# Filling every SBUF pool up to a multiple of 256 bytes in a four-layer fp32r transformer kernel

## The chip, the cores and the metric

The kernel runs on one core of a Trainium2 chip. The metric is the device time of one execution in microseconds. Three runs of the kernel before took 4075.82, 4077.94 and 4079.65 us; their median, 4077.94 us, is the time before. Another execution was profiled; durations below are of that one.

## The reference

The kernel computes four transformer layers over 1024 rows of 1024 float32 values, one after the other: a layer of dilated window attention and a layer of multi-head latent attention (MLA), each with an adaptive scale, shift and gate from `c` and a layernorm behind it, and then two layers of a second block. Cut to the second block, in which most of the time lies:

```python
for l in range(2):
    h = rms_norm(x, norm_mix_pre[l])
    proj = h @ w_in[l]                       # 1024x1024 @ 1024x2560
    q_da, k_da, v_da, q_r, k_r, v_r, g_r, u_pool = jnp.split(proj, split_points, axis=-1)
    o_da = diff_attention(q_da, k_da, v_da, ...)   # 4 heads, two causal softmaxes subtracted
    o_ret = retention(q_r, k_r, v_r, g_r, ret_norm[l])
    o_pool = pool_mixer(u_pool, pool_w[l], pool_scale[l])
    mix = jnp.concatenate([o_da, o_ret, o_pool], axis=-1) @ w_out[l]   # 1024x1024
    x = x + rms_norm(mix, norm_mix_post[l])
    h = rms_norm(x, norm_mlp_pre[l])
    u = h @ w_up[l]                          # 1024x1024 @ 1024x5632
    uc = conv_b + sum(conv_w[j] * up[:, j:j + S] for j in range(3))   # up: u, two rows of zeros ahead
    gate, val = jnp.split(uc, 2, axis=-1)
    y = (gelu(gate) * val) @ w_down[l]       # 1024x2816 @ 2816x1024
    x = x + rms_norm(y, norm_mlp_post[l])
```

## The kernel before

**Products.** All large products are made from fp32r tiles. A float32 operand is split into a high part (`uh`, `wh`, `hh`, `yh`) and the rest (`ul`, `wl`, `hl`, `yl`), and a product is three matmuls into the same PSUM tile: high by low, high by high, low by high (`PASSES`). A matmul takes a stationary operand of up to 128 columns and a moving one of up to 512; in the trace's `out<-a,b` the first, `a`, is the stationary one. All matmuls go through `mm` (L151), transposes through `tr` (L156, with the identity `ident`).

**Stages.** `build` (L1889) runs phase A (dilated attention), phase B (MLA), and then twice `phase_mix` (projections, differential attention, retention, pooling, and the output product in `mix_tail`, L1666) and `phase_mlp` (L1740). The transposed activations of a stage are in a `UT` object (L98): `uh0`, `uh1`, `ul0`, `ul1`, each 128 x 4 x 8 x 128, named by the stage in which they are made: `uh_a` for dilated attention, `uh_n` for MLA and for the first mix layer, `uh_f` for the second, `uh_m` for the MLPs. In the MLP the up projection makes two halves of 512 rows per 128 columns of `w_up` (products `y<-uh_m,wh` or `g<-uh_m,wh`, 24 matmuls each, with the PSUM tags `y` and `g` in turn); the down projection, in groups of four 128-row pieces of `w_down`, takes `hh`/`hl` as the moving operand or the stationary one and the weights `wh`/`wl` as the other. TensorE's order in the MLP is written out by `pin` (each instruction is kept in program order); elsewhere the scheduler orders each engine's instructions.

**Memory.** A tile comes from a pool. Pools are opened and closed as on a stack, on the left side of each partition's SBUF (upward from its bottom) or on the right side (downward from its top), so a pool's address follows from the sizes of all pools open before it on that side. Left: `const` (the identity and other constants; opened first), `wraw` (raw weights `wr`), `ut`, and then a stage's own. Right: among others `pw` (L1895, three buffers for each of `wh` and `wl`), which holds the weights of both mix layers and both MLPs. A `TagPool` (L122) is a family of such pools, one for each tag, opened at a tag's first tile or by `reserve`. No size is rounded beyond 32 bytes, so small tiles (statistics, vectors of constants) shift all that is opened behind them.

**Queues.** Nearly all transfers are issued on the SP queue, in one order that the scheduler sets; a transfer waits for its data, its buffer and the ones ahead of it on the queue. In `mix_tail`, `load` fetches a piece `yr` of the stored mixer outputs `mixd`, which earlier stores (`mixd<-do` of differential attention, L1602) wrote.

Of the kernel before, what the change touches and what calls it, by code (L numbers as in the profile page):

```python
# [12 lines left out]
F32 = mybir.dt.float32  # L13
# [8 lines left out]
P = 128  # L22
# [75 lines left out]
class UT:  # L98


    def __init__(self, k, name):
        self.hi = [k.ut.tile([P, 4, KT, P], F32R, tag=f"uh{h}", name=f"uh{h}_{name}") for h in range(2)]
        self.lo = [k.ut.tile([P, 4, KT, P], F32R, tag=f"ul{h}", name=f"ul{h}_{name}") for h in range(2)]
# [4 lines left out]
    def lhs(self, part, t, kt):  # L108
        return (self.hi if part == 0 else self.lo)[t // 4][:, t % 4, kt, :]


class Pools:


    def __init__(self, rest, tags):
        self.rest, self.tags = rest, tags

    def tile(self, shape, dtype, **kw):
        return self.tags.get(kw.get("tag"), self.rest).tile(shape, dtype, **kw)


class TagPool:  # L122


    def __init__(self, k, ctx, name, bufs, side):
        self.k, self.ctx, self.name, self.bufs, self.side, self.pools = k, ctx, name, bufs, side, {}

    def reserve(self, *tags):
        for t in tags:
            self.pools[t] = self.k.pool(self.ctx, f"{self.name}_{t}", bufs=self.bufs, side=self.side)  # L130

    def tile(self, shape, dtype, **kw):
        t = kw.get("tag") or kw["name"]
        if t not in self.pools:
            self.reserve(t)
        return self.pools[t].tile(shape, dtype, **kw)


PASSES = ((1, 0), (0, 0), (0, 1))


class Kern:
# [26 lines left out]

    def tags(self, ctx, name, bufs=1, side="left"):  # L170
        return TagPool(self, ctx, name, bufs, side)

    def psum(self, ctx, left="", right=""):

        for side, tags in (("left", left), ("right", right)):
            for t in tags:
                self.ps.tags[t] = self.pool(ctx, "ps" + t, space=PSUM, side=side)
# [62 lines left out]
    def gemm_T_half(self, w, ut, half, ps, cols=slice(0, P), kts=range(KT)):  # L240
        for kt in kts:
            for n, (a, b) in enumerate(PASSES):
                self.mm(ps, w[kt][a][:, cols], ut.rhs(b, half, kt), start=(kt == 0 and n == 0),
                        stop=(kt == KT - 1 and n == 2))

    def gemm_N(self, ps, w, cols, lhs, kts=KT):
# [3 lines left out]
        for kt in range(kts):  # L250
            for a, b in PASSES:
                self.mm(ps, lhs(b, kt), w[kt][a][:, cols], start=(m == 0), stop=(m == 3 * kts - 1))
# [58 lines left out]
    def setup(self, ctx):  # L311
        nc = self.nc
        self.cp = self.pool(ctx, "const")
        self.wr = self.pool(ctx, "wraw")
        self.ut = self.pool(ctx, "ut")
        self.dr = self.pool(ctx, "dram", space=DRAM)
        self.ident = self.cp.tile([P, P], F32, name="ident")
        make_identity(nc, self.ident)
        self.xs = [self.dr.tile([S, D], F32, name=f"xs{j}") for j in range(2)]
        self.modd = self.dr.tile([4, 1024], F32, name="modd")  # L320
# [612 lines left out]
    def mla_heads(self, ctx, cr, lat, kbuf, rope, sgd, yT, rd, begin_tail):  # L933
# [27 lines left out]
        def quad_v(qd, t, ps):  # L961
            _, wv, vt, _ = quad[qd]
            ps = ps[:, :256].rearrange("p (h e) -> p h e", h=4)
            for n, (a, b) in enumerate(PASSES):
                self.mm(ps, lat[b][:, 2, t * P:(t + 1) * P], wv[a][:, 1], start=(n == 0), stop=(n == 2))
            self.split(vt[:, t, :, 0:64], vt[:, t, :, 64:128], ps)

        def pair_k(qd, pr, half, ps=None):
            wv = quad[qd][1]
            hs = slice(half * 512, (half + 1) * 512)  # L970
            ps = self.pp("g", 1) if ps is None else ps
            for n, (a, b) in enumerate(PASSES):
                self.mm(ps, wv[a][:, 0, pr * 2:pr * 2 + 2], lat[b][:, 2, hs], start=(n == 0), stop=(n == 2))
# [153 lines left out]
    def tail_finish(self, ctx, early, late, w_out, x_res, layer):  # L1127
# [7 lines left out]
        with ctx:  # L1135
# [22 lines left out]
            def product(t, side):  # L1158
# [8 lines left out]
                for j, (ks, rows) in enumerate(parts):  # L1167
# [5 lines left out]
                    for kt in ks:  # L1173
                        for n, (a, b) in enumerate(PASSES):
                            for h in range(2):
# [56 lines left out]
    def phase_mix(self, l, ut, x_res):  # L1232
        nc, i = self.nc, self.i
        w_in = i["w_in_2"][l]
        mixd = self.dr.tile([S, 1024], F32, name=f"mixd{l}")
        with ExitStack() as ctx:
            cw = ExitStack()
            wn = self.pw
            dp = self.tags(ctx, "dae")
            dp.reserve("dv0", "dv1", "dconst", "dc", "rp0", "rp1", "rp2", "rp3")  # L1240
            self.psum(cw, "tg")
            c1 = ExitStack()
            self.psum(c1, "", "xsv")
            rest = self.retention(self.tags(c1, "rt"), dp, wn, l, ut, w_in, mixd)

            def late_pool():
                c1.close()
                self.up = ExitStack()
                self.psum(self.up, "", "y")
                return self.tags(ctx, "da")  # L1250

            def begin_tail():
                w = self.load_w(wn, i["w_out_2"][l, 512:], 0, 1024, 3, cut=4)
                return w, {}, {}, []

            def load_y(early, h):
                y0 = early[1][h] = self.raw([P, 2, 512])
                nc.sync.dma_start(y0, mixd[:2 * P, h * 512:(h + 1) * 512].rearrange("(t p) n -> p t n", p=P))

            def turn_y(early, t, h):  # L1260
                yy = self.wr.tile([P, 2, 4, P], F32R, tag="wr", bufs=5, name=self.nm("wr"))
                tp = self.pp("g", 2, [P, 4, P])
                self.transposes(tp, early[1][h][:, t], 4)
                self.split(yy[:, 0], yy[:, 1], tp)
                early[2][t, h] = yy[:, 0], yy[:, 1]

            def products(early, t):
                w, _, yy, ps = early
                ps.append(self.pp("y", 2, [P, 1024]))
                self.out_product(ps[t], yy[t, 1], w, range(3), start=True)  # L1270

            def end(early, n):

                if n == -2:
                    load_y(early, 1)
                elif n in (-1, 0):
                    turn_y(early, n + 1, 1)
                    if n == 0:
                        load_y(early, 0)
                elif n in (1, 2):  # L1280
                    turn_y(early, n - 1, 0)

            early = self.diff_attention(dp, wn, l, ut, w_in, mixd, rest, late_pool, begin_tail, end, products)
        return self.mix_tail(cw, early, l, mixd, x_res)
# [40 lines left out]
    def retention(self, lp, dp, wn, l, ut, w_in, mixd):  # L1325
# [13 lines left out]
        def proj_pool(ti, half):  # L1339
            ps = self.pp("g", 2)  # L1340
            n = 0
            for kt in range(KT):
                for a, b in PASSES:
                    self.mm(ps, w_pool[ti][kt][a], ut.rhs(b, half, kt),
# [573 lines left out]
```

## Time and profile before

| | |
|---|---|
| median of three runs | 4077.94 us |
| profiled execution | 4074.51 us, span of its instructions 4072.7 us |
| mean granted TensorE clock | 0.978 of full speed |
| TensorE (PE) busy | 3848.7 us, 95% of the span, 21088 matmuls |
| VectorE (DVE) busy | 2455.7 us, 60% |
| ScalarE (ACT) busy | 1381.1 us, 34% |
| GpSimd (POOL) busy | 1089.9 us, 27% |
| DMA | 290.78 MB, mean 71 GB/s |

Busy time is that in which at least one instruction of an engine runs; matmuls are pipelined, so a printed duration holds the fill and drain of the array, and overlaps the next one's. What a matmul costs in a row of them is the distance from one start to the next. Times in the trace count from the start of the span. Stages: dilated attention to about 800 us, MLA to about 1551, mix layer 0 to 2028, its MLP to about 2820, mix layer 1 to 3306, its MLP to the end. PEclk is the granted clock of TensorE: 1.00 is 2.4 GHz, 0.50 is 1.2 GHz.

### The profile page before, as it was taken

The numbers are of one execution on the slowest core, as the hardware profiler recorded it, in microseconds if no ns is written. First come the engines' busy times: TensorE is split into PE (matmuls) and PEld (weight loads), VectorE is DVE, ScalarE is ACT, GpSimd is POOL, SyncE is SP. The second block draws the span as 40 slices with busy tenths as digits, with TensorE's granted clock in tenths as the row PEclk, the third lists the DMA queues.
The fourth block names the chain that finished last, engine by engine and source line by source line (L and its number), as shares of the span: only waits on it lengthen the run. The fifth ranks groups of instructions, "written<-read, shape, count | busy, mean of one in ns | idle before, by whom it ended". The sixth has DMA issues, their size and how long they took to land. (4 is left out here: it accounts for less than half of the span.)

```text
span 4072.7 us, 54330 instructions
## 1 busy us (share of the span) xinstructions
PE 3848.7 (95%) x21088; PEld 3265.4 (80%) x21088; DVE 2455.7 (60%) x4599; ACT 1381.1 (34%) x2938; POOL 1089.9 (27%) x1016
## 2 busy tenths in 40 slices
PE   7999998899999899999999999997999999999998
PEld 5778776788889778998778888886999778888886
DVE  6655567938887766588744444438568754343436
ACT  3434341127777532265311111113246431111111
POOL 1121212311122222233232222234134232323233
PEclk9999999999999999999999999998999999999999
DMA  6333324320111342101421111113111331111112
GB/s 239 99 93 81 100 68 149 90 71 17 28 36 30 93 126 86 42 30 53 142 70 47 47 47 47 47 52 115 47 45 37 117 98 42 52 42 52 42 52 83
DMA packets 300367, 290.78 MB, mean 71 GB/s; under 512 B 52107, under 2 KB 254739, under 8 KB 300110
## 3 DMA queue, kind: packets, MB, share of 16 engines
q1 hardware_dynamic: 294834, 268.23, 21.7%
q10 hardware_dynamic: 5276, 19.08, 1.6%
q8 instruction: 167, 2.74, 0.3%
q14 instruction: 90, 0.74, 0.1%
HBM read 240.26 MB, written 51.72 MB: 72 GB/s over the span
## 5 line engine op out<-in xcount | busy, mean ns | idle before, releaser
L203 POOL TENSOR_TENSOR wl<-wr,wh 128x1024 fp32r<-128x1024 f32 (+1 forms) x253 | 498.2, 1977 | 1461.5 <-DVE wh L199 1393.6
L199 DVE CAST wh<-wr 128x1024 fp32r<-128x1024 f32 x222 | 181.6, 819 | 688.9 <-PE y L151 312.4
L151 PE MATMUL y<-uh_m,wh 128*128 128x512 f32 x1056 | 420.4, 398 | 0.0
L151 PE MATMUL y<-uh_m,wl 128*128 128x512 f32 x1056 | 417.9, 396 | 2.2 <-DVE z L1643 1.7
L151 PE MATMUL y<-ul_m,wh 128*128 128x512 f32 x1056 | 419.2, 397 | 0.0
L1796 ACT ACTIVATE cv<-y,cw 128x1024 f32<-128x1024 f32 x66 | 79.8, 1209 | 776.9 <-PE y L151 776.9
L151 PEld LDWEIGHTS y<-uh_m,wl 128*128 128x128 f32 x1056 | 199.3, 189 | 52.5 <-DVE z L1643 2.2
L151 PEld LDWEIGHTS y<-uh_m,wh 128*128 128x128 f32 x1056 | 199.5, 189 | 48.7
L151 PEld LDWEIGHTS y<-ul_m,wh 128*128 128x128 f32 x1056 | 199.4, 189 | 47.6 <-DVE ul_m L191 0.7
L151 PE MATMUL g<-uh_a,wl 128*128 128x512 f32 x568 | 233.3, 411 | 0.2 <-ACT uh_a L419 0.2
L151 PE MATMUL y<-wo,yh 128*128 128x512 f32 x784 | 217.6, 400 | 15.6 <-ACT yh L1170 15.4
L151 PE MATMUL g<-ul_a,wh 128*128 128x512 f32 x568 | 226.6, 399 | 0.5 <-POOL ul_a L422 0.4
L151 PE MATMUL g<-uh_a,wh 128*128 128x512 f32 x568 | 225.6, 397 | 0.0
L151 PEld LDWEIGHTS y<-wo,yh 128*128 128x128 f32 x784 | 147.8, 191 | 48.4 <-issue 14.5
L191 DVE TENSOR_TENSOR pt<-t,pt 128x512 fp32r<-128x512 f32 x256 | 165.9, 681 | 22.5 <-ACT pt L190 20.8
L151 PE MATMUL y<-wl,hh 128*128 128x512 f32 x440 | 175.0, 398 | 0.0
L151 PE MATMUL y<-wh,hh 128*128 128x512 f32 x440 | 174.8, 397 | 0.0
L151 PE MATMUL y<-wh,hl 128*128 128x512 f32 x440 | 174.6, 397 | 0.0
L1007 DVE TENSOR_REDUCE nm<-s 128x1 f32<-128x1024 f32 x128 | 155.7, 1216 | 26.5 <-PE s L151 25.9
L151 PE MATMUL g<-wl,uh_n 128*128 128x256 f32 x576 | 166.1, 288 | 3.4 <-DVE dv L191 2.9
L151 PE MATMUL g<-wl,uh_f 128*128 128x256 f32 x576 | 166.1, 288 | 3.1 <-DVE dv L191 2.6
L151 PE MATMUL v<-pt,v 128*64 128x256 f32 (+1 forms) x1024 | 154.9, 294 | 11.1 <-DVE o L1042 11.0
(451 smaller groups left out, 10275.9 us busy)
## 6 DMA issues: line engine op xcount, KB each, us to landing
wr<-w_up SPq DMA_DIRECT2D x88, 512.0 KB, 3.9
wr<-ada_w SPq DMA_DIRECT2D x48, 512.0 KB, 5.5
wr<-w_down SPq DMA_DIRECT2D x44, 512.0 KB, 3.5
wr<-a_w_in SPq DMA_DIRECT2D x36, 512.0 KB, 4.5
wr<-w_in SPq DMA_DIRECT2D x24, 512.0 KB, 3.6
xs<-wr SPq DMA_DIRECT2D x16, 512.0 KB, 2.6
wr<-xs ACTq DMA_DIRECT2D x16, 512.0 KB, 3.7
wr<-w_in SPq DMA_DIRECT2D x32, 256.0 KB, 3.0
```

Source lines behind the costliest of these rows:

```text
L151: ins = self.nc.tensor.matmul(*args, **kw)
L191: nc.vector.tensor_tensor(lo, src, hi.bitcast(F32), OP.subtract)
L199: (self.nc.scalar.copy if act else self.nc.vector.tensor_copy)(hi, raw)
L203: (eng or self.nc.gpsimd).tensor_tensor(lo[..., cs], raw[..., cs], hi[..., cs].bitcast(F32), OP.subtract)
L1007: nc.vector.tensor_reduce(nm, sp, AX.X, OP.max, negate=True)
L1796: nc.scalar.activation(t, ps, AF.Identity, bias=cw[:, 3, c:c + 1], scale=cw[:, 2, c:c + 1])
```

## The change

Each pool of a `TagPool` is given a neighbour, `..._fill`, which holds one unused tile, as large as is missing from the pool's size to the next multiple of 256 bytes. Behind the constants on the left lies a fill of 192 bytes (`LEFT`), at the top on the right one of 224 (`RIGHT`), and one pool that is reserved but gets small tiles of its own sizes (`dconst`) has its fill written out, 224.

```diff
--- before.py
+++ after.py
@@ -122,21 +122,30 @@
 class TagPool:
 
 
+
     def __init__(self, k, ctx, name, bufs, side):
         self.k, self.ctx, self.name, self.bufs, self.side, self.pools = k, ctx, name, bufs, side, {}
+        self.fill = {}
 
     def reserve(self, *tags):
         for t in tags:
             self.pools[t] = self.k.pool(self.ctx, f"{self.name}_{t}", bufs=self.bufs, side=self.side)
+            self.fill[t] = self.k.pool(self.ctx, f"{self.name}_{t}_fill", side=self.side)
 
     def tile(self, shape, dtype, **kw):
         t = kw.get("tag") or kw["name"]
         if t not in self.pools:
             self.reserve(t)
+        fill = self.fill.pop(t, None)
+        if fill:
+            size = -(-math.prod(shape[1:]) * 4 // 32) * 32 * kw.get("bufs", self.bufs)
+            self.k.fill(fill, -size % ROUND)
         return self.pools[t].tile(shape, dtype, **kw)
 
 
 PASSES = ((1, 0), (0, 0), (0, 1))
+ROUND = 256
+LEFT, RIGHT = 192, 224
 
 
 class Kern:
@@ -169,6 +178,11 @@
 
     def tags(self, ctx, name, bufs=1, side="left"):
         return TagPool(self, ctx, name, bufs, side)
+
+    def fill(self, pool, size):
+
+        if size:
+            pool.tile([P, size // 4], F32, name=self.nm("fill"))
 
     def psum(self, ctx, left="", right=""):
 
@@ -311,6 +325,8 @@
     def setup(self, ctx):
         nc = self.nc
         self.cp = self.pool(ctx, "const")
+        self.fill(self.pool(ctx, "left"), LEFT)
+        self.fill(self.pool(ctx, "right", side="right"), RIGHT)
         self.wr = self.pool(ctx, "wraw")
         self.ut = self.pool(ctx, "ut")
         self.dr = self.pool(ctx, "dram", space=DRAM)
@@ -1238,6 +1254,7 @@
             wn = self.pw
             dp = self.tags(ctx, "dae")
             dp.reserve("dv0", "dv1", "dconst", "dc", "rp0", "rp1", "rp2", "rp3")
+            self.fill(dp.fill.pop("dconst"), 224)
             self.psum(cw, "tg")
             c1 = ExitStack()
             self.psum(c1, "", "xsv")
```

What it does to the addresses, as the built programs have them, bytes past a multiple of 256 at which a tile starts:

| tiles | before | after |
|---|---|---|
| `uh`, `ul` of all stages; `wr`; `hh`, `hl`; MLA's `kb`, `qh`, `ql`, `pt`, `v` | 64 | 0 |
| `wh`, `wl` of dilated attention and of MLA's gates (left) | 64 | 0 |
| `wh`, `wl` of both mix layers and both MLPs (`pw`, right) | 224 | 0 |
| `wo` and `yh`, `yl` at the end of dilated attention (right) | 224 and 224 | 0 and 0 |
| `wo` and `yh`, `yl` at the end of MLA (left) | 64 and 64 | 0 and 0 |
| `wo` and `yh`, `yl` of `mix_tail` (left) | 64 and 192 | 0 and 0 |
| `wh`, `wl` with `yh`, `yl` made by `turn_y` ahead of `mix_tail` | 224 and 64 | 0 and 0 |
| `dk` and `dq` of differential attention | 96 and 96 | 0 and 0 |
| `dv` and `dp` of differential attention | 64 and 0 or 96 | 0 and 0 |
| MLA's 416-column weights `wb` with `uh`, first and second half | 224, 96 with 64 | 0, 128 with 0 |
| `ident` (float32, with 128-column operands) | 128 | 128 |

Offsets within a tile are multiples of 512 bytes in all the 512-column products. Of these there are 11232 in fp32r; in 4128 both operands start at the same offset before, in 7104 they don't. After the change both start at 0 in all of them.

The instructions of TensorE, VectorE and ScalarE are the same, in the same order; on GpSimd two `memset`s change places. On the SP queue the order differs in three places. The first is in `mix_tail` of the first mix layer, where `yr` is a piece of `mixd` for one 128-row tile and `do` an output of differential attention. Before:

```order
L1684 DMA yr_20945<-mixd_14936 128x512
L1602 DMA mixd_14936<-do_20267 128x4x128
L1684 DMA yr_20734<-mixd_14936 128x512
L1684 DMA yr_20867<-mixd_14936 128x512
L1684 DMA yr_20994<-mixd_14936 128x512
```

After:

```order
L1701 DMA yr_21526<-mixd_15424 128x512
L1701 DMA yr_21665<-mixd_15424 128x512
L1701 DMA yr_21743<-mixd_15424 128x512
L1619 DMA mixd_15424<-do_20960 128x4x128
L1701 DMA yr_21792<-mixd_15424 128x512
```

Two `yr` loads now stand ahead of the store instead of behind it. The second place is the same spot of the second mix layer, with the same move. The third is where the second mix layer loads its tables (`rdec`, `rxz` for retention, `dcrope` and `dcgs` for differential attention; `wr` are raw pieces of `w_in`). Before:

```order
L1379 DMA rdec<-k_decay 128x512
L1456 DMA dcrope<-k_rope 128x128
L217 DMA wr_26664<-w_in 128x4x256
L217 DMA wr_26973<-w_in 128x4x256
L206 DMA dcgs<-diff_subln 128x128
L1381 DMA rxz<-k_xizeta 128x256
```

After:

```order
L1473 DMA dcrope<-k_rope 128x128
L220 DMA dcgs<-diff_subln 128x128
L231 DMA wr_27590<-w_in 128x4x256
L231 DMA wr_27912<-w_in 128x4x256
L1398 DMA rxz<-k_xizeta 128x256
L1396 DMA rdec<-k_decay 128x512
```

`rdec` has gone from the head of the six to their end, and `dcgs` ahead of the two weight loads.

## Rows read from the trace of the kernel before

**Rows 1.** Stages by window: busy us (xcount) of each engine, PEclk, DMA share, GB/s.

```profile
10.00:33.00 23.00, 14.25 (x51) 8.68 (x52) 19.45 (x17) 6.32 (x11) 0.00 (x0) 0.90 1.05 381
...
1551.00:1722.00 171.00, 163.79 (x1276) 158.34 (x1276) 97.30 (x269) 33.95 (x99) 35.56 (x37) 0.98 0.18 55
...
2028.00:2768.00 740.00, 734.64 (x3144) 589.58 (x3143) 317.42 (x331) 114.55 (x111) 222.17 (x93) 1.00 0.17 53
...
3306.00:4015.00 709.00, 704.15 (x3007) 565.57 (x3006) 291.58 (x280) 106.54 (x100) 206.55 (x86) 1.00 0.17 51
```

**Rows 2.** Chain of waits, a piece in the last MLP: start, us, what.

```profile
3349.90 22.40 PE y L151 x96
```

**Rows 3.** Timeline of PE, start of the first MLA block: start, us, instruction.

```profile
825.70 0.39 PE L151 MATMUL g<-ul_n,wh 128*128 128x512 f32 x1
...
831.82 0.39 PE L151 MATMUL g<-ul_n,wh 128*128 128x512 f32 x1
```

**Rows 4.** Timeline of PE, start of the first mix layer.

```profile
1576.75 0.40 PE L151 MATMUL g<-ul_n,wh 128*128 128x512 f32 x1
...
1585.85 0.40 PE L151 MATMUL g<-ul_n,wh 128*128 128x512 f32 x1
```

**Rows 5.** Stretches inside stages by window, same columns as the first group.

```profile
825.00:895.00 70.00, 70.00 (x310) 57.99 (x309) 15.11 (x24) 10.94 (x17) 16.21 (x8) 1.00 0.23 76
1560.00:1584.00 24.00, 24.00 (x170) 22.35 (x169) 18.60 (x55) 2.92 (x8) 9.52 (x6) 1.00 0.26 78
2060.00:2760.00 700.00, 700.00 (x2997) 562.78 (x2997) 290.26 (x270) 103.26 (x95) 204.62 (x86) 1.00 0.16 49
```

**Rows 6.** Timeline of PE, `wo` products: dilated block, then first mix tail.

```profile
629.83 0.62 PE L151 MATMUL y<-wo,yh 128*128 128x512 f32 x2
...
641.17 0.61 PE L151 MATMUL y<-wo,yl 128*128 128x512 f32 x2
...
1975.19 1.08 PE L151 MATMUL y<-wo,yh 128*128 128x512 f32 x4
1976.12 0.62 PE L151 MATMUL y<-wo,yl 128*128 128x512 f32 x2
```

**Rows 7.** PE by line and shape: xcount, busy us, mean ns, idle before, releaser.

```profile
L151 PE MATMUL y<-uh_m,wh 128*128 128x512 f32 x1056 | 420.4, 398 | 0.0
...
L151 PE MATMUL y<-wh,hh 128*128 128x512 f32 x440 | 174.8, 397 | 0.0
...
L151 PE MATMUL g<-wl,uh_n 128*128 128x256 f32 x576 | 166.1, 288 | 3.4 <-DVE dv L191 2.9 <-POOL wl L203 0.5
...
L151 PE MATMUL g<-uh_m,wh 128*128 128x512 f32 x352 | 139.6, 396 | 0.0
...
L151 PE MATMUL g<-wh,hh 128*128 128x512 f32 x264 | 104.6, 396 | 0.0
...
L156 PE MATMUL g<-ident,yr 128*128 128x128 f32 x96 | 14.4, 273 | 1.0 <-DMA yr<-mixd 0.6 <-issue 0.4
```

**Rows 8.** Timeline of PE, 256 columns: MLA values, then first mix layer.

```profile
1099.82 0.63 PE L151 MATMUL v<-pt,v 128*64 128x256 f32 x4
1100.29 0.39 PE L151 MATMUL s<-kb,ql 96*128 96x512 f32 x1
...
1569.77 0.28 PE L151 MATMUL g<-wh,ul_n 128*128 128x256 f32 x1
...
1575.46 0.28 PE L151 MATMUL g<-wh,ul_n 128*128 128x256 f32 x1
```

**Rows 9.** Timeline of the SP queue, loads in the first mix tail.

```profile
1945.92 5.50 SPq L1684 DMA_DIRECT2D yr<-mixd  x3
```

**Rows 10.** Timeline of PE, end of the first MLP, clock at half.

```profile
2795.27 0.63 PE L151 MATMUL y<-wh,hl 128*128 128x512 f32 x1
...
2796.13 0.61 PE L151 MATMUL y<-wh,hh 128*128 128x512 f32 x1
```

## The prediction, made before the changed kernel ran

> **What bounds the kernel now.** I read the table of stages first [rows 1]. In the long stages the reader is to see TensorE busy almost without a break: 734.64 us of 740 and 704.15 of 709 in the two MLP stages, 163.79 of 171 in the first differential-attention projections, while VectorE, ScalarE and GpSimd each stand below half of the MLP stages. The chain of waits says the same of the last MLP: it runs through matmul after matmul, 96 of them in 22.40 us, 233.3 ns each [rows 2]. So the time of one matmul, times some thousands, is the time of the kernel, and a change that alters no instruction can count only through what one instruction takes.
>
> The second view is the timeline of TensorE, read by the distance from one start to the next (the printed durations overlap and don't show it). The reader is to see that the same product, `g<-uh_n,wl / uh_n,wh / ul_n,wh`, 128x128 by 512 columns, has two speeds. At the start of the first MLA block 27 distances take 831.82-825.70 = 6.12 us, **226.7 ns** each [rows 3]; at the start of the first mix layer 39 take 1585.85-1576.75 = 9.10 us, **233.3 ns** [rows 4]. The granted clock is 1.00 in both [rows 5]. What differs by the table of addresses above: in the first stretch both operands start 64 bytes past a multiple of 256; in the second the `uh` operand starts at 64 and the weight at 224. I take "same offset" and "different offsets" as two classes. Two more rows bear that out with other tiles: `wo` with `yh`/`yl` of the dilated block, both at 224, take 641.17-629.83 = 11.34 us for 50, 226.8 ns [rows 6]; those of a mix tail, at 64 and 192, 0.93 us for 4, 232.5 ns [rows 6]. And the whole middle of the first MLP, where all pairs are 64 with 224, gives 700.00/2997 = 233.6 ns [rows 5].
>
> **The change part by part.** It adds no instruction to any engine. It moves SBUF addresses, and through them a few SP loads.
>
> *512-column products.* By the addresses, 7104 of 11232 stand in the different class before; after, all stand in the same class. By groups [rows 7]: `uh_m` with weights, 3 x 1056 and 3 x 352 (up projection); weights with `hh`/`hl`, 3 x 440 and 3 x 264 (down projection): 6336. The rest of the built program's pairs: 96 `uh_f`, 96 `uh_n`, 216 `wl/wh` with `yh/yl`, 72 with `wr`: together 6816 at 64/224. Taking 233.4 - 226.7 = 6.7 ns each: 45.7 us. Then 288 `wo` pairs at 64/192, 232.5 - 226.8 = 5.7 ns: 1.6 us. Sum 47.3. Of it 6336 lie in MLP stages where TensorE waits 5.4 and 4.8 us in all [rows 1]; the few per cent in the tails may be lost to waits, so I count **46.3 us**. The cover that could take it back there is another engine: VectorE, busiest of them, has 317.42 of 740 us and would stand at 317 of some 718, so none is late next.
>
> *256-column products.* 3456 pairs of weights with `uh` [rows 7] go from 224/64 to the same class, and 288 `dv,dp` too. In the different class 48 distances take 5.69 us, 118.5 ns; in the same class (`pt,v`, both at 64) 4 take 0.47 us, 117.5 ns [rows 8]. By the rows' two decimals the difference is 1.0, give or take 2.5 ns. These stages wait for VectorE for a part (97.30 of 171 us busy, TensorE 163.79 [rows 1]), so of 3744 x 1.0 = 3.7 us I take **2 us**. The bounds are 0 and 3744 x 3.5 = 13 us, where every pair gains the most that the rows leave room for.
>
> *416- and 384-column, 128-column products.* 192 of 416 columns change, half of them to a difference of 128 bytes; 192 x 6.7 = 1.3 us is the most, 0 the least; I take 0, since half keep different offsets. The 128-column ones with `ident` still differ by 128 after: 0.
>
> *Loads past the stores on SP.* In both mix tails two `yr` loads of t = 2 and 3 go ahead of a `mixd<-do` store. Before, three loads come at 1945.92 and land by 5.50 us later [rows 9]; the transposes that read `yr` cost TensorE 1.0 us of idle time over both layers [rows 7], and that is the most to be had: 0 to 1.0, I take **0.5**. Behind the moved loads on SP stands the store and then a `yr` load that is read after three more tiles; nobody is waiting for it. The three small table loads that change places at the start of the second mix layer are read by retention long after the projections: 0, at most the 1 us or so that one load takes.
>
> *Transfers and other engines.* Tiles now begin on multiples of 256. The one stretch full of transfers is 10 to 33 us, DMA share 1.05 [rows 1]; in the MLP the share is 0.17, hidden. If each 4 KB row lost a seventeenth of its time, 23/17 = 1.4 us; the least is 0, and I take 0. VectorE, ScalarE and GpSimd I cost at 0: they are hidden in the MLP with over 400 us to spare each.
>
> Sum: 46.3 + 2 + 0.5 = 48.8 us off the profiled execution's 4074.5: 4025.7. The three runs have their median 3.4 us above it (4077.94), so **4029 us** as a median.
>
> A rule against this, weighed: rows 3 and 4 show one product at 226.7 and 233.3 ns at one granted clock. The Trainium skill, page "SBUF — State Buffer", section "SBUF: two separate sides", says that TensorE, with ports of its own (a second one for loading weights), never waits on anyone there, and gives no price of an operand's offset; its section "Operand start alignment" is on what is legal and says that its runs timed nothing. By it the change would give nothing; the two speeds speak against it, unless they have another cause, which is rival A.
>
> **The rivals.**
> A. *The two speeds belong to the stage, not to the offsets*: other engines' reads or transfers slow the matmuls, or the right side of the memory, where the slow weights lie. Then nothing moves: 4077 us (the 0.5 us of loads aside). For it: every 64/224 pair has one operand on the left and one on the right. Against: the `wo,yh` pairs of a mix tail both lie on the left and take 232.5; 233.3 and 233.6 come with VectorE busy 18.60 of 24 us and 290.26 of 700, 78% and 41%, and 226.7 with 22% [rows 5]: no proportion. DMA shares are 0.26, 0.16 and 0.23: the fastest is not the emptiest.
> B. *Slower*: offset 0 itself is bad. No 512-column pair starts on a multiple of 256 before, so both operands at 0 was never seen. If two streams that start on the same boundary collide at every 256 bytes, the changed pairs stay at 233.4 and the 4128 that now run at 226.7 pay 6.7 ns as well: +27.7 us, nearly all on TensorE's path, some 4104 us. It decides as soon as the distance at the start of MLA goes from 226.7 up to 233. Against: 64/64 and 224/224 cost the same, so the place within 256 didn't matter when both shared it.
> C. *More than forecast*: the offset also causes the rest. With the clock granted at half, 1.2 GHz, matmuls start 2796.13-2795.27 = 0.86 us for two [rows 10], about 427 ns, which is 512 columns at that clock; at 2.4 GHz that would be 213.3, so 13.4 ns of the fast class are not columns. If starting on 256 takes them away as well, 11232 x 13.4 = 150 us more: about 3880. A quarter of it would be near 3990. For it: nothing but that the 13.4 ns exist. Against: 64 and 224 leave them alike.
>
> **How the numbers follow.** Forecast 0.82, A 0.07, B 0.04, C (in whole or part) 0.07. The range holds the forecast with its unknowns: up to 11 us more from 256 columns and 2.7 more from the small terms, with 4 us for the reading of distances to 0.01 us: 4011. The other way, 2.5 us less from the two small terms, and if a tenth to a fifth of the 46 us turns into waits, 9 us: 4041. 4011 to 4041, which leaves out A, B and C with 0.18. A measurement of this kernel can tell about 0.2%, 8 us, from no change. Faster by more: forecast and C, 0.89; within: A, 0.07; slower: B, 0.04.
>
> **What would show it.** In the changed profile: distances of 226 to 227 ns in both mix layers' `g<-uh_n` and over the whole MLP (its middle, 2997 matmuls, about 680 us in place of 700); MLA and the dilated block unchanged; MLP stages shorter by about 21 us each with the same idle time; clock as before. 233 in the MLP proves A, 233 in MLA proves B, anything clearly under 226 proves C. The forecast is also wrong if distances fall but the stages don't: then a wait has come in.

## The result and the profile after

The changed kernel takes 4036.82 us (median of four runs, 4034.73 to 4037.68), the kernel before beside it 4076.88 (4075.22 to 4079.65): a ratio of 0.990, 95% interval 0.9883 to 0.9917. 40 us were gained where 48.8 had been forecast, and the time lies inside the range. The profiled execution took 4036.28 us against 4074.51.

One correction to the text ahead first: in `out<-a,b` of the trace the moving operand stands first and the stationary one second, not the other way round. So in the up projection (`uh_m,wh`) the activations stream and the weights are loaded; in the mix layers' 256-column products (`wl,uh_n`) the weights stream and the activations are loaded. No number of the prediction rests on it, since only the difference of the two offsets counts in it.

The page of the kernel after: span and TensorE's busy time, and groups of the matmuls that answer to [rows 7].

```profile
span 4034.3 us, 54328 instructions
...
PE 3812.4 (94%) x21088; PEld 3276.5 (81%) x21088; DVE 2455.2 (61%) x4599; ACT 1380.0 (34%) x2938; POOL 1089.5 (27%) x1016
...
L160 PE MATMUL y<-uh_m,wh 128*128 128x512 f32 x1056 | 413.0, 391 | 0.0
...
L160 PE MATMUL g<-wl,uh_n 128*128 128x256 f32 x576 | 167.5, 291 | 3.0 <-DVE dv L205 2.5
```

The first group's mean fell from 398 to 391 ns, the 7 ns that were forecast. The second rose from 288 to 291: the 256-column products became slower. VectorE, ScalarE and GpSimd are busy as long as before, to 1.1 us; no other engine took part.

Next the middle of the first MLP by window, and two pieces of the chain of waits in the last MLP (the second answers to [rows 2]):

```profile
2100.00:2700.00 600.00, 600.00 (x2649) 496.99 (x2648) 250.62 (x219) 83.77 (x74) 176.63 (x74) 1.00 0.16 49
```

```profile
3907.96 10.88 PE g L160 x48
3918.84 21.76 PE y L160 x96
```

600.00/2649 = 226.5 ns where [rows 5] gave 233.6, and 21.76/96 = 226.7 where [rows 2] gave 233.3. From the same matmul to the same matmul, 428 distances in the middle of either MLP take 97.0 us instead of 100.0, 7.0 ns less each.

The start of MLA, where both operands stood at 64 and now stand at 0 (27 distances), and 60 distances of 256 columns at the start of the first mix layer:

```profile
825.75 0.39 PE L160 MATMUL g<-uh_n,wh 128*128 128x512 f32 x1
...
831.87 0.39 PE L160 MATMUL g<-uh_n,wh 128*128 128x512 f32 x1
```

```profile
1558.78 0.28 PE L160 MATMUL g<-wh,ul_n 128*128 128x256 f32 x1
...
1565.98 0.28 PE L160 MATMUL g<-wh,ul_n 128*128 128x256 f32 x1
```

6.12/27 = 226.7 ns, what [rows 3] gave: equal offsets at 0 are neither worse (rival B) nor better (rival C) than equal offsets at 64. But 7.20/60 = 120.0 ns in the 256-column products, where [rows 8] had 118.5.

Where the time went, each stretch taken from the start of one matmul to the start of the same one in the other traces (us). The columns "again" are second traces of the same two kernels, from the last experiment:

| stretch | before | before again | after | after again |
|---|---|---|---|---|
| dilated attention, its projections (to 628) | 624.95 | 620.30 | 625.14 | 625.95 |
| its end and MLA (628 to 1551) | 922.85 | 914.24 | 920.09 | 916.10 |
| mix layers up to their tails | 726.96 | 727.30 | 733.54 | 733.64 |
| the two mix tails | 225.99 | 226.91 | 224.93 | 223.76 |
| the two MLPs | 1552.24 | 1551.90 | 1510.91 | 1509.07 |

Each of the two lines before 1551 moves by up to 8.6 us between two traces of one kernel, so nothing can be read from them. The other three lines repeat within 0.9 us in the kernel before and 1.8 in the changed one, and tell the story: MLPs 41 to 43 us down, mix layers 6.5 us **up**, tails 1 to 3 us down.

### The profile page after: what moved, and what is told of

Same layout as the page of the kernel before. It is cut to its first block, busy times and chain, and to the rows that moved or that the text cites. A ratio compares the mean times of both kernels' runs of the same rounds, so it can differ in the third digit from the quotient of the medians.

```text
span 4034.3 us, 54328 instructions
## 1 busy us (share of the span) xinstructions
PE 3812.4 (94%) x21088; PEld 3276.5 (81%) x21088; DVE 2455.2 (61%) x4599; ACT 1380.0 (34%) x2938; POOL 1089.5 (27%) x1016
## 5 line engine op out<-in xcount | busy, mean ns | idle before, releaser
L160 PE MATMUL g<-ul_a,wh 128*128 128x512 f32 x568 | 226.5, 399 | 0.5 <-POOL ul_a L438 0.4
L160 PE MATMUL g<-wh,ul_n 128*128 128x256 f32 x576 | 165.3, 287 | 0.0
```

The source lines that it names most:

```text
L160: ins = self.nc.tensor.matmul(*args, **kw)
```

## The experiments

In all of them the instructions, and their order on the engines, are those of one of the two kernels, and only addresses move (in mix224 and mix32 GpSimd has one stretch of `memset`s and weight splits in another order). 512-column distances below are means over the MLPs, 256-column ones over the mix layers, from the starts in each trace, at full clock and within unbroken rows of matmuls.

**Which offset counts.** Four kernels change one line of the changed kernel:

```diff
-LEFT, RIGHT = 192, 224
+LEFT, RIGHT = 0, 160     # both64
+LEFT, RIGHT = 192, 64    # r160
+LEFT, RIGHT = 192, 96    # r128
+LEFT, RIGHT = 192, 192   # r32
```

> Both sides of the memory moved by 64 bytes, so all that started at a multiple of 256 now starts 64 past one, and every pair still has the same offset. If only the difference of the two offsets counts, nothing moves against the changed kernel: 512-column distances 226.7 ns in the MLP, 256-column ones 119.8 ns in the mix layers, about 4037 us. If a start at 0 is what made the 256-column products slower, they go back to 118.2 ns, 3456 x 1.6 = 5.5 us, about 4031 us. If a start at 0 is what made the 512-column products faster, the MLP goes back to 233.5 ns and the time to about 4075 us.

> The changed kernel with the right side moved, so that weights in the mix layers and MLPs start at 160 and the activations at 0: the difference that they had before, at other absolute offsets, with every pool still filled up. If the difference counts: MLP distances 233.4 ns, 256-column ones 118.2 ns, 6336 x 6.8 = 43 us more and 5.5 less, about 4074 us. If the filling as such (round pool sizes, left and right) made the gain, the MLP stays at 226.7 and the time near 4037 us.

> As before but right side at 128, left at 0. By the difference alone the MLP should take what the mix tail took before with 64 and 192, 232.5 ns: 6336 x 5.8 = 37 us more than the changed kernel, about 4070 us. If any difference costs the same 6.7 ns: 233.4 ns and about 4075 us. For the 256-column products no value is known; between 117.4 and 120 ns.

> Right side at 32, left at 0: the smallest difference that the pools allow. If equality is what counts (a step), MLP distances are 233 ns and the time about 4075 us. If the price grows with the difference (a slope), 32 bytes of 160 cost a fifth: 228 ns, 8 us more than the changed kernel, about 4045 us; the 256-column products would then stay near 119.8 ns, with a step they fall to 118.2.

| kernel | weights, activations start at | 512 columns, ns | 256 columns, ns | median us | ratio to before (95%) |
|---|---|---|---|---|---|
| before | 224, 64 | 233.6 | 118.1 | 4072.48 | 1 |
| changed | 0, 0 | 226.7 | 119.9 | 4036.82 | 0.990 (0.9883 to 0.9917) |
| both64 | 64, 64 | 226.7 | 119.9 | 4035.52 | 0.991 (0.9894 to 0.9924) |
| r160 | 160, 0 | 233.6 | 118.3 | 4067.05 | 0.999 (0.9976 to 0.9995) |
| r128 | 128, 0 | 233.3 | 118.9 | 4068.53 | 0.999 (0.9978 to 0.9997) |
| r32 | 32, 0 | 233.3 | 116.8 | 4064.69 | 0.998 (0.9974 to 0.9992) |

(The before of 4072.48 is the one that ran beside the four; the changed kernel ran beside another, so compare ratios.) The middle of the first MLP by window in both64 and, in the second fence, in r32:

```profile
2100.00:2700.00 600.00, 600.00 (x2649) 496.93 (x2648) 252.69 (x221) 83.78 (x74) 175.77 (x74) 1.00 0.16 49
```

```profile
2100.00:2700.00 600.00, 600.00 (x2573) 482.73 (x2572) 245.26 (x214) 80.39 (x71) 172.82 (x72) 1.00 0.16 47
```

2649 matmuls in 600 us when both start at 64, as many as at 0; 2573 when one of them is moved by 32 bytes, with the pools filled up exactly as in the changed kernel. What counts for 512 columns is that the two offsets are equal. It is a step, not a slope: 32 bytes cost 6.6 ns, 160 cost 6.9. That 256 bytes is the right measure of "equal" can be seen too: by the addresses of the built programs, nearly all MLP pairs of both64 start an odd multiple of 256 bytes apart and all of the changed kernel a multiple of 512, and both take 226.7 ns, while 128 bytes apart (r128) takes 233.3. Rival A (stage, side, other engines) falls with it, since between r32 and the changed kernel nothing else differs. For 128 bytes I had expected 232.5 from the mix tails; it is 233.3.

The 256-column products go the other way. With equal offsets they take 119.9 ns at 64 as at 0, so a start at 0 isn't the cause; with unequal ones 116.8 to 118.9. Of the differences in this table the smallest is the best.

**Is the filling of pools needed?** The kernel before with one tile more:

```diff
         self.cp = self.pool(ctx, "const")
+        self.pool(ctx, "right", side="right").tile([P, 40], F32, name="fill")
```

> The kernel before with nothing but one unused tile of 160 bytes at the top of the right side, so that the weights of both mix layers and MLPs start at 64 like the activations; no pool is filled up. If the difference between the two operands is all, this does what the whole change does: MLP distances 226.7 ns, 256-column ones 119.8 ns, mix tails (64 with 192, left alone) 232.5 ns, about 4038 us where the changed kernel has 4037. If round pool sizes have a share of their own, it stays above that by their share.

4036.42 us, ratio 0.992 (0.9905 to 0.9934); 512 columns 226.7 ns, 256 columns 119.9. The same window:

```profile
2100.00:2700.00 600.00, 600.00 (x2649) 496.99 (x2648) 250.42 (x219) 83.74 (x74) 176.80 (x74) 1.00 0.16 49
```

These 160 bytes do what the whole change does, within the intervals; a share of the filling itself can't be told from nothing.

**Both optima at once.** The changed kernel, with the stationary operand of the 256-column products moved alone:

```diff
+U_OFF = 224     # mix224; 32 in mix32
...
-        self.hi = [k.ut.tile([P, 4, KT, P], F32R, tag=f"uh{h}", name=f"uh{h}_{name}") for h in range(2)]
-        self.lo = [k.ut.tile([P, 4, KT, P], F32R, tag=f"ul{h}", name=f"ul{h}_{name}") for h in range(2)]
+        o = U_OFF // 4 if name in ("n1", "f0") else 0
+        n = 4 * KT * P
+
+        def tile(tag):
+            t = k.ut.tile([P, n + 64], F32R, tag=tag, name=f"{tag}_{name}")
+            return t[:, o:o + n].rearrange("p (t k c) -> p t k c", t=4, k=KT)
+
+        self.hi = [tile(f"uh{h}") for h in range(2)]
+        self.lo = [tile(f"ul{h}") for h in range(2)]
```

> The changed kernel with only the activations of the two mix layers moved to 224 (their tiles are 256 bytes larger), so that the 256-column products have a moving operand 32 bytes past the stationary one, and the MLPs keep equal offsets. If the difference has the opposite effect on 256 columns, their distance falls from 119.8 to 116.8 ns as in the run with the right side at 32: 3456 x 3.0 = 10 us, less 192 x 6.6 = 1 us for the 512-column products of the same activations, and with waits some 6 to 9 us under the changed kernel, about 4029 us. If 116.8 came from something else in that run, 119.8 stays and the time is 4037 to 4039 us.

> The same with the activations at 32: the stationary operand 32 bytes past the moving one. If only the size of the difference counts: 116.8 ns as with 224. If its sign counts, as an order of two streams: another value, between 117 and 120 ns. 512-column products of these activations 233 ns either way.

mix224: 4022.33 us, ratio 0.989 (0.9875 to 0.9912). mix32: 4025.72, 0.989 (0.9880 to 0.9909). 256 columns take 116.9 ns in the first and 118.3 in the second, so the sign of the difference counts too: it is better when the moving operand stands 32 bytes past the stationary one than 32 short of it. 512 columns stay at 226.7 in both. 61 distances of mix224:

```profile
1558.82 0.28 PE L168 MATMUL g<-wl,uh_n 128*128 128x256 f32 x1
...
1565.94 0.28 PE L168 MATMUL g<-wh,uh_n 128*128 128x256 f32 x1
```

7.12/61 = 116.7 ns, and the mix layers up to their tails take 725.28 us, 8 less than in the changed kernel. This profiled execution was the slowest of its four runs (4034.23 us, the others 4020.51 to 4023.56), so the trace shows the gain of the mix layers but not that of the whole kernel.

**Whose offset a matmul pays for.** The low weight parts alone, moved in the right side's pool:

```diff
-            self.k.fill(fill, -size % ROUND)
+            self.k.fill(fill, -size % ROUND + {("pw", "wh"): 32, ("pw", "wl"): 224}.get((self.name, t), 0))
```

> The changed kernel with only the low parts of the weights in the right side's pool (wl) moved to 224, the high parts (wh) left at 0. In the up projection three matmuls follow one another: uh with wl, uh with wh, ul with wh; the moving operand is at 0 in all three. If a matmul pays for its own stationary operand's offset, the distance after uh,wl is 233 ns and the other two are 226.7. If it pays for the operand that is loaded while it streams, the next one's, the distance after ul,wh is 233 ns. Either way about 1408 x 6.7 = 9.4 us more in the MLPs than the changed kernel; the 256-column products with wl change too, by 0 to 3 us. About 4045 us.

Neither of the two alone. Of the up projection's three distances, the one after `uh,wh` (own weights at 0, next at 0) is 227.2 ns, after `uh,wl` (own at 224, next at 0) 231.7, after `ul,wh` (own at 0, the next one's at 224) 234.7: means of 1388, 1388 and 1370. Together they make the MLPs 17.8 us longer than in the changed kernel, where one alone had been put at 9.4; the 256-column products gain a part of it back, 118.6 ns on average. 4041.77 us, ratio 0.993 (0.9916 to 0.9949). The weight loads beside the matmuls, first the loads, then the matmuls:

```profile
2199.90 0.19 PEld L160 LDWEIGHTS y<-uh_m,wl 128*128 128x128 f32 x1
2200.13 0.19 PEld L160 LDWEIGHTS y<-uh_m,wh 128*128 128x128 f32 x1
```

```profile
2199.89 0.40 PE L160 MATMUL y<-ul_m,wh 128*128 128x512 f32 x1
2200.13 0.39 PE L160 MATMUL y<-uh_m,wl 128*128 128x512 f32 x1
2200.36 0.39 PE L160 MATMUL y<-uh_m,wh 128*128 128x512 f32 x1
2200.59 0.40 PE L160 MATMUL y<-ul_m,wh 128*128 128x512 f32 x1
```

The load of `wl` for the next matmul begins as `ul_m,wh` starts to stream, and that matmul, whose own two operands are both at 0, takes 7.5 ns longer than the one between 0 and 0. So the address of the next weights alone changes how long a matmul takes, with its own two operands equal. The 4.5 ns after `uh_m,wl` aren't explained: by the rows its weights have been loaded (2199.90 + 0.19) before it starts (2200.13). The two figures aren't prices that add up, either: in r160, where own and next weights both stand 160 past the activations, a distance is 6.9 ns above equality, not 7.5 and 4.5 together. In the down projection, where the weights stream, a `wl` at 224 over a stationary `hh` at 0, with the next one at 0 too, takes 233.6 ns (64 distances): again 6.9 in all.

The Trainium skill, page "TensorE: Matmul & The Clock Gate", section "Step-by-step: what each phase is for", says: "Loading the next tile's weights doesn't steal SBUF read bandwidth from the running matmul." The trace doesn't agree: 234.7 against 227.2 ns at one granted clock (1.00), by the address of the next weights.

**The same two kernels again, and the shortest version.** On one chip: the kernel before, the changed one and mix224 once more, and the kernel before with only the 160 bytes and the `U_OFF = 224` tiles, no pool filled up (the two diffs above).

> The kernel before, unchanged, profiled a second time, to see how far a stage's time and the number of matmuls at half clock move without any change. If the forecast's last 2 to 4 us were lost to the change, this trace has again about 110 of the 512-column distances at 427 ns and the same time in each stage within 0.5 us; if they are scatter, it has other counts (the runs so far have 110 to 152) and stages that differ by 1 to 3 us.

> The changed kernel, unchanged, on the same chip as the other three: MLP distances 226.7 ns, 256-column ones 119.8 ns; a ratio of 0.990 to the kernel before.

> The changed kernel with the mix layers' activations at 224, again, beside the changed kernel on the same chip: 8 to 14 us under it, a ratio of 0.987 to 0.988 to the kernel before.

> The kernel before with two edits only: one unused tile of 160 bytes at the top of the right side, and the mix layers' activations 224 bytes further on in tiles that are 256 bytes larger, so at 32 where the weights are at 64. No pool is filled up. If equal offsets for 512 columns and 32 bytes for 256 columns are all there is to gain, it is as fast as the version before this one, within 3 us: MLP distances 226.7 ns, 256-column ones 116.8 ns. If the filling of pools has a share (the mix tails' 288 pairs are 1.6 us of it), it is slower by that.

| kernel | 512 columns, ns | 256 columns, ns | median us | ratio to before (95%) |
|---|---|---|---|---|
| before again | 233.6 | 118.1 | 4069.65 | 1.000 (0.9992 to 1.0011) |
| changed again | 226.7 | 119.9 | 4031.77 | 0.991 (0.9893 to 0.9926) |
| mix224 again | 226.7 | 116.8 | 4019.46 | 0.988 (0.9868 to 0.9899) |
| two edits | 226.7 | 116.9 | 4026.52 | 0.989 (0.9879 to 0.9909) |

mix224 has the lowest medians of all, 12 us under the changed kernel on this chip and 47 to 50 under the kernel before. Its interval and that of the changed kernel just overlap; that there is a gain is told by the 256-column distances and the mix layers' 726.01 us (725.57 in two edits) against 733.64. The profiled execution was again the slowest of its four (4029.64, the others 4017.20 to 4019.75), and against the changed kernel's trace beside it 4.7 us more in the MLPs and 2.7 before 1551 take the mix layers' 7.6 back; what made the other three faster by more than the mix layers give isn't shown. Two edits has 4026.52 where mix224 has 4019.46, but their intervals overlap widely, its MLPs are not the longer ones (1511.54 against 1513.76 us), and the profiled executions stand the other way round (4024.88 and 4029.64), so no trace shows where the 7 us lie. Whether the filling is worth some microseconds there stays open.

The core's span in the two traces of the kernel before, the first in the table ahead of the prediction (4072.7 us), the second:

```profile
core 0: 4060.3 us, clock 0.978
```

12 us apart without any change, all of it before 1551: the two lines there moved by 4.7 and 8.6 us, the three others by at most 0.9. That is neither of the answers expected, since the count of distances at half clock is the same, 110 and 108.

## Why the prediction came out as it did

**The main step was right.** The two speeds of one product were read as equal and unequal offsets, and priced at 6.7 ns x 6336 = 42.5 us in the MLPs. Measured: 41.3 us in the first pair of traces, 42.8 in the second, with distances of 226.7 ns as at the start of MLA. r32 and both64 show the cause and not only the size: 32 bytes undo it, moving both sides together doesn't. The two classes named only a matmul's own operands, though; wlo224 adds the weights that are loaded beside it.

**The term that failed is that of the 256-column products**: 2 us of gain, bounds 0 and 13 us of gain. The mix layers up to their tails, where these products run, lose 6.6 us (6.3 in the second pair), and 3456 x 1.8 ns = 6.2 us says the same; against the 2 us of gain that makes 8.6 of the 10.6 us by which the profiled execution (38.2 us down) misses the sum (48.8). The step behind it took the value of equal offsets from `pt,v`, short runs of 8 matmuls at 117.5 ns [rows 8], and carried over from 512 columns that equal is better. `pt,v` is another shape: half of its stationary operands have 64 columns (`128*64`), and it takes 117 ns in the changed kernel as before; whether the width or the short runs set it apart wasn't tried. In the long runs of the mix layers equal offsets give 120 ns nearly every time (within 0.6 ns in 92% of the distances; 27% before), unequal ones nine times in ten between 115 and 122, with a mean of 118.1. (The shares are of distances inside longer rows.) A loss should have been among the bounds: rows 8 differed by less than their rounding, and nothing excluded the other sign.

**Chance had a part in the total.** The stages from 1551 on gave 35.8 us in the first pair of traces and 39.6 in the second. Nearly all the rest of the two differences, 2.6 us for the changed kernel in the first pair and 7.5 against it in the second, lies before 1551, where the two traces of the kernel before differ by 13.3 us.

**The tails gave less than they should.** 288 pairs at 5.7 ns, 288 more at 6.7 ns and 0.5 us for the `yr` loads are 4.0 us; 1.1 and 3.2 were measured. The moved loads did what was forecast: SP issues the first three between 1934.11 and 1937.49 us, where before two of them came behind the store, at 1945.92 and 1946.29, and the transposes' idle time before `yr` went from 1.0 us [rows 7] to none. (The 3.38 us of the row below, like the 5.50 of [rows 9], is the time from the first issue to the end of the last, not to the landing, as the prediction read it; the median from issue to landing of the `yr` loads is 4.2 us before and 4.7 after. The sum used only the 1.0 us.)

```profile
1934.11 3.38 SPq L1701 DMA_DIRECT2D yr<-mixd  x3
```

```profile
L165 PE MATMUL g<-ident,yr 128*128 128x128 f32 x96 | 14.4, 272 | 0.0
```

At full clock the `wo` pairs went from 232.7 to 228.5 ns and the 288 others from 234.3 to 229.2, not to 226.8 and 226.7: 4.2 and 5.1 ns each, 2.7 us where 3.5 had been counted. In the first pair of traces the clock took most of the rest back: in the tails 14 and 8 of the 512-column distances stand at half clock in the two traces of the changed kernel, 0 and 7 in those of the kernel before, 0.2 us each. The other traces have between 0 (mix32) and 16 (wlo224) there, so nothing ties them to equal offsets. The first MLP shows one such place as well, after a wait of 1.81 us for ScalarE:

```profile
2047.25 1.09 PE L165 MATMUL t<-ident,u 128*128 128x128 f32 x8 [1.81 <-ACT u L1673]
...
2049.60 0.63 PE L160 MATMUL y<-ul_m,wh 128*128 128x512 f32 x1
...
2051.31 0.62 PE L160 MATMUL y<-uh_m,wl 128*128 128x512 f32 x1
```

Four distances of 427 ns at a granted clock of 0.50 (2049.2 to 2051.7 us), where the trace before, after a wait of 1.80 us at the same place, has 1.00. Over the first MLP the counts are 24 against 15 in the first pair and 24 against 23 in the second, which at 0.2 us each is most of why it gave 19.2 us in one and 21.2 in the other. Over the whole kernel the traces of before have 110 and 108 such distances, all others some 120 to 152; 31 to 60 of each lie in dilated attention; whether the other addresses have a part in that or only chance wasn't tried.

**The steps at zero held.** No engine but TensorE became slower or faster, the transfers of the filled stretch (10 to 33 us) kept their share of 1.05, the 416-column products take 188.9 ns after 188.4, and no wait took the MLPs' gain: VectorE, which would have been next, was never reached.

**The rivals.** A is refuted by r32 and r160, B and C by both64 and the start of MLA. The Trainium skill's rule that stood for A (page "SBUF — State Buffer", section "SBUF: two separate sides": TensorE never waits on anyone) may hold between engines, on which no run here bears; within TensorE, wlo224 shows that a matmul's time depends on the weight load beside it. That the change does more than is needed was not among the rivals and should have been: 160 bytes in one place give the same.

## What to carry to other kernels

Read a matmul's cost from start to start and group it by where the operands begin within 256 bytes: here 512-column fp32r products take 226.7 ns when moving and stationary operand, and the next one's weights, begin at the same place, and 233 when weights and activations differ throughout: 3% of their time hangs on the order of some pools. It takes no rounding of every pool, only one unused tile that brings the two sides into step. Don't carry an optimum over to another width: the 256-column products of the mix layers want the opposite, and both can be had by moving one operand inside its tile.

## What the runs showed of the hardware that I had not expected

- In long rows with 128-column stationary operands the width reverses the sign: equal offsets save 6.9 ns of 512 columns (233.6 to 226.7) and cost 1.8 ns of 256 (118.1 to 119.9); 32 bytes between moving and stationary operand cost 6.6 and save 3.1 against equality.
- The difference has a direction for 256 columns: +32 bytes 116.9 ns, -32 bytes 118.3.
- A matmul of 512 columns whose own operands are equal takes 7.5 ns longer when the weights that are loaded while it streams stand at another offset (wlo224); the matmul over those weights, 4.5. Where all differ it is 6.6 to 6.9, so these don't add.
- Even at equal offsets the 512-column distances of the MLPs' long rows average no less than 226.7 ns in any run. 512 columns at 2.4 GHz are 213.3. The Trainium skill's page "TensorE: Matmul & The Clock Gate", section "Wait — 56ns, not 53.3ns?", gives 215.7 for back-to-back matmuls at that clock. The 11 ns between aren't explained by these runs; that they vanish at half clock, where distances are 427 ns, speaks for reads that can't keep up at full clock, which is argued, not shown.
